# FFN2's activation block sums on GpSimd instead of VectorE, its weight sums on VectorE from two plain loads

## The chip, the cores and the metric

The kernel runs on one core of a Trainium2 chip. The metric is the device time of one execution in microseconds, as a median of several. The core has five engines that run on their own and wait for each other by semaphores: TensorE (PE in the profile), VectorE (DVE), ScalarE (ACT), GpSimd (POOL) and SyncE (SP), which only issues DMAs here.

## The reference

One layer of a hybrid decoder on 1024 tokens of width 1024 (16 meta tokens are put in front). The change touches only the last product.

```
u = rmsnorm(h, g_pre_mix);  z = u @ w_in                 # q | k | v | x | y
attn = sliding_window_attention_with_sinks(q, k, v)      # window 128
rec  = gelu(y) * rg_lru(conv(x))
h = h + rmsnorm(concat(attn, rec) @ w_out, g_post_mix)
u = rmsnorm(h, g_pre_ffn)
f = square(relu(u @ w_ff1)) @ w_ff2                      # w_ff1 1024x4096, w_ff2 4096x1024
h = h + rmsnorm(f, g_post_ffn)                           # returned without the meta tokens
```

## The kernel before, in words

All large products are made in three passes: a float32 operand is split into a high half and a low half (both in the format fp32r), and `mm3` adds high x high, high x low and low x high in PSUM (lines 124, 125 and 126). `split` makes the halves: ScalarE copies the operand into the high half (line 95), VectorE subtracts that from the operand for the low half (line 98).

FFN2 (`w_ff2`) is done by a scheme that replaces eight block products by seven. The activations are kept as four blocks, `fb["11"]`, `["12"]`, `["21"]` and `["22"]`, each of eight tiles 128x(2x512), and `w_ff2` is cut into four blocks in the same way. Each of the seven rows of `PLAN` names which activation blocks are added or subtracted (a single name, or two and an operation), which weight blocks, and into which halves of the result (`facc`) the product goes with which sign. A row is a product `i` from 0 to 6, and it has eight steps `q`, one for each 512 rows of the inner dimension. So there are 56 steps. In each, TensorE makes 24 matmuls of 128x128 by 512 columns (four accumulators of one PSUM bank each, for four groups of 128 tokens, two slices of the inner dimension, three passes); `q` = 7 finishes a product. Block sums of the activations stand in products 0, 1, 2, 5 and 6. Weight sums stand in products 1 to 4 and 6, as ADD in 1, 2 and 6 and as SUB in 3 and 4.

For step `n` the kernel does this ahead:

- `fetch_2(n)`, three steps ahead: the one or two weight blocks are loaded, 512 KB each, into a slot with the tag `raw` and one with the tag `e`, in turns (two slots of each tag). Plain loads are issued by SP (line 1125). For most steps with ADD (`q % 3 < 2` in products 1 and 2, `q` in 0, 2, 4 in product 6) the second block is not loaded into a slot of its own: GpSimd issues a DMA that adds it to the first in memory (`accum_op=ADD`, line 1122).
- `prep_2(n)`, one step ahead: where two blocks were loaded, VectorE combines them (`combine`, line 861). The weight is split into a pair with the tag `ws` (four slots, that is two steps; the last three steps use slots with the tag `a`). Where the plan asks for it, VectorE makes the activation sum, also by `combine`, into a slot with the tag `b`, which is then split into two more slots of that tag. There are 17 slots with the tag `b`, part of which are held by the activation blocks and by `facc`.
- `step_mm` runs the matmuls. The last three steps (`LAST`) are run group by group of tokens instead.

When a product is done, `evict` adds its four accumulators to `facc`, one each in the first four steps of the next product: a first write goes by ScalarE, a later one by VectorE (a sum of a PSUM bank and an SBUF tile of 128x512, line 861). In products 5 and 6 the finished rows are normalized and added to the output: `finish_early` (ScalarE squares, GpSimd a power for the reciprocal root, `rs`, line 169, VectorE a product, line 1191, GpSimd an accumulating DMA to the output, line 1195), `finish_half` and, at the end, `finish_late` (its last product on GpSimd is line 1244, its reductions on VectorE are line 1229, its output DMAs on GpSimd line 1238).

The order of the instructions on each engine is not written out. A list scheduler with a model of the chip's times makes it when the program is built, from the dependences, the slots of the pools and a few ordering hints (`behind`). After that each engine works through its own fixed order, so an instruction that waits holds up all that stand behind it on its engine.

Of the kernel before, what the change touches and what calls it, by code (L numbers as in the profile page):

```python
# [37 lines left out]
def hybrid_layer(  # L38
# [6 lines left out]
    nc = tc.nc  # L45
# [12 lines left out]
    def slot(tag, shape, dt=F32):  # L58
        uid[0] += 1
        return slab.tile(shape, dt, tag=tag, name=f"{tag}{uid[0]}", bufs=bufs[tag])  # L60

    def pair(tag, shape):
        return slot(tag, shape, F32R), slot(tag, shape, F32R)
# [29 lines left out]
    def split(hi, lo, src, eng=None):  # L93
        if eng is None:
            nc.scalar.copy(hi, src)  # L95
        else:
            eng.tensor_copy(hi, src)
        low = nc.vector.tensor_tensor(lo, src, f32(hi), op=ALU.subtract).ins  # L98
        mark[0] = low.name
        return low  # L100
# [4 lines left out]
    def behind(name, *inss):  # L105
        for ins in inss:
            tc.add_manual_dep(
                ins, name,
                mybir.DependencyInfo(
                    mybir.DependencyClass.NoSync, mybir.DependencyReason.DATA  # L110
                ),
                reason="order",
            )
# [157 lines left out]
    def high_w(raw, tag="ws"):  # L271
        hi, lo = pair(tag, [P, KC, P])
        chained(0, nc.scalar.copy(hi, raw).ins)
        return hi, lo
# [59 lines left out]
    wx = high_w(rx)  # L334
# [525 lines left out]
    def combine(dst, x0, x1, op):  # L860
        return nc.vector.tensor_tensor(dst, x0, x1, op=op).ins  # L861
# [79 lines left out]
    fb = {k: [None] * 8 for k in ("11", "12", "21", "22")}  # L941
# [158 lines left out]
    w2v = w_ff2.rearrange("(q s a p) (b c) -> q a b p s c", s=2, a=2, p=P, b=2)  # L1100
    ADD, SUB = ALU.add, ALU.subtract
# [11 lines left out]
    def fetch_2(n):  # L1113
        i, q = steps[n]
        wx = PLAN[i][1]
        tags = (("raw", "e"), ("e", "raw"))[n % 2]
        raws = []
        for (a, b), tag in zip(wx[:2], tags):
            if len(wx) == 3 and wx[2] is ADD and raws and (
                q % 3 < 2 if i < 6 else q in (0, 2, 4)  # L1120
            ):
                nc.gpsimd.dma_start(raws[0], w2v[q, a, b], accum_op=ADD)  # L1122
                break
            r = slot(tag, [P, 2, 512])
            nc.sync.dma_start(r, w2v[q, a, b])
            raws.append(r)
        return raws

    def prep_2(n, tag="ws"):
        i, q = steps[n]  # L1130
        fx, wx, _ = PLAN[i]
        raws = raw_2.pop(n)
        if len(raws) == 2:
            ins = combine(raws[0], raws[0], raws[1], wx[2])
            if i == 6:
                behind(w_low[0], ins)
        wh, wl = pair(tag, [P, 2, 512])
        w_low[0] = split(wh, wl, raws[0]).name
        if len(fx) == 3:
            f = slot("b", [P, 2, 512])  # L1140
            combine(f, fb[fx[0]][q], fb[fx[1]][q], fx[2])
        else:
            f = fb[fx[0]][q]
        fh, fl = pair("b", [P, 2, 512])
        split(fh, fl, f)
        return fh, fl, wh, wl
# [9 lines left out]
    for n, p in enumerate(third):  # L1156
        if n + 2 < 16:
            raw_c[third[n + 2]] = fetch_c(third[n + 2])
        if n >= 13:
            raw_2[n - 13] = fetch_2(n - 13)  # L1160
        if n + 1 < 16:
            wc[third[n + 1]] = prep_c(third[n + 1])
        if n == 15:
            ready[0] = prep_2(0)
        if p not in a12_early:
            y2 = bank(("acc", "s")[p % 2])
            product(y2, wc[p][0], ob21, True)
            nc.vector.tensor_tensor(block("11", p), y2, block("11", p), op=ALU.add)
        y4 = bank(("pt", "o")[p % 2])
        if n == 0:  # L1170
            product_by_parts(y4, wc[p][1], ot4)
        else:
            product(y4, wc[p][1], ot4, True)
        nc.vector.tensor_tensor(block("21", p), y4, block("21", p), op=ALU.add)
        done.add(p)
        if p ^ 1 in done:
            activate("11", p // 2)
            activate("21", p // 2)
# [110 lines left out]
    for n, (i, q) in enumerate(steps):  # L1289
        if n + 3 < len(steps):  # L1290
            raw_2[n + 3] = fetch_2(n + 3)
        if n + 1 < len(steps):
            late = w_low[0]
            ready[n + 1] = prep_2(n + 1, "a" if n + 1 >= len(steps) - LAST else "ws")
        if q == 0:
            old = None if i == 0 else accs
            accs = [[bank(("acc", "s", "pt", "o")[j])] for j in range(4)]
            if i == 6:

                evict(5, 0, old[0][0], late)  # L1300
                accs[3] = [accs[3][0][:, :256], bank("acc")[:, :256]]
        if n < len(steps) - LAST:
            for j in range(4):
                for acc, cols in zip(accs[j], col_parts(i, j)):
                    step_mm(acc, j, q, ready[n], cols)
            del ready[n]
        if old and (q > 0 or i < 6) and q < 4:
            evict(i - 1, q, old[q][0], late)
        if i == 5 and q == 0:
            gffn_b = slot("a", [P, D])  # L1310
            nc.scalar.dma_start(gffn_b, g_post_ffn[0].partition_broadcast(P))
        if (i, q) in EARLY:
            finish_early(EARLY.index((i, q)))
        if i == 6 and 1 <= q < 5:
            finish_half(q - 1)
        if i == 6 and q == 4:
            root = small.tile([P, 1], F32, name="root", tag="root")
            lut(root, half_pow, AF.Sqrt, scale=-1.0)
# [36 lines left out]
```

## Time and profile before

| | |
|---|---|
| median of 3 runs | 976.04 us (975.72 to 976.45) |
| the profiled execution | 983.92 us, its span 982.2 us |
| TensorE clock granted, mean | 0.991 of full speed |
| busy share of the span: PE, PEld, DVE, ACT, POOL | 97%, 81%, 67%, 51%, 14% |
| HBM read, written | 110.46 MB, 18.87 MB |

The profiled execution is slower than the runs by 0.8%; numbers from the trace are compared among themselves. FFN2's matmuls run from about 661 us to 972 us of the span. In the rows of the profile, `out<-in` are the names of the tiles without their numbers: `ws<-raw,ws` on line 98 is the low half of a weight, `b<-b,b` on line 98 the low half of an activation sum, `b<-a,c` on line 861 an activation sum, `e<-e,raw` and `raw<-raw,e` on line 861 a weight sum, `b<-ps_pt,b` an eviction. A time in brackets is idle time of the engine just before the instruction, with what ended it. "Chain" is the chain of work that ended last, followed back from the end.

### The profile page before, as it was taken

To read this page: it belongs to the slowest core of one execution; us is meant where nothing else is said; L and a number is where in the kernel's file an instruction comes from. 1 tells how busy PE (TensorE), PEld (TensorE's weight loads), DVE (VectorE), ACT (ScalarE), POOL (GpSimd) and SP (SyncE) were. 2 spreads that over 40 slices of the span, in tenths; PEclk is the share of its full clock that TensorE was granted. 3 is DMA by queue.
4 is the path that set the end of the run, shared out by engine and by line. 5 is a ranking of instruction groups with operands and counts; after the bars stand their busy time and mean duration, and the time that the engine had idled before them with its cause. 6 is when DMAs were issued, how large, how long until landed. Compare 5 with 4: busy or idle time off the path is not lost.

```text
span 982.2 us, 12324 instructions
## 1 busy us (share of the span) xinstructions
PE 951.9 (97%) x4654; PEld 797.1 (81%) x4654; DVE 662.9 (67%) x942; ACT 500.5 (51%) x816; POOL 140.3 (14%) x184
## 2 busy tenths in 40 slices
PE   6999989999899999999999999999999999999996
PEld 6998988888788887887788888888888788888885
DVE  5569976755876687656554455468567666779885
ACT  6556562548935554343455556555433343445432
POOL 4016753230002100000000000000011000003011
PEclk9999989999999999999999999999999999999999
DMA  8111001112234465575532264423678766656653
GB/s 282 49 46 42 22 23 44 33 43 65 86 107 150 150 215 192 172 243 192 187 129 86 85 200 121 129 86 108 164 180 194 166 222 207 177 168 150 168 175 85
DMA packets 84794, 131.30 MB, mean 134 GB/s; under 512 B 5464, under 2 KB 48616, under 8 KB 84736
## 3 DMA queue, kind: packets, MB, share of 16 engines
q1 hardware_dynamic: 76912, 109.55, 34.7%
q0 software_dynamic: 7248, 19.40, 9.7%
q10 hardware_dynamic: 576, 1.57, 0.4%
q8 instruction: 36, 0.59, 0.3%
q14 instruction: 22, 0.18, 0.1%
HBM read 110.46 MB, written 18.87 MB: 132 GB/s over the span
## 4 chain that ended last, share of the span: by engine, by line
PE 80%; DVE 7%; ACT 5%; DMA 3%; issue 3%; POOL 2%; DVEq 0%; SPq 0%; ACTq 0%; POOLq 0%
PE ps_acc L124 8%; PE ps_acc L125 8%; PE ps_acc L126 8%; PE ps_pt L125 6%; PE ps_pt L126 6%; PE ps_pt L124 6%; PE ps_s L126 6%; PE ps_s L125 6%; PE ps_s L124 6%; PE ps_o L125 5%; PE ps_o L124 5%; PE ps_o L126 5%; DMA d<-in_w_ff_dram 2%; ACT c L82 1%; DVE ws L98 1%
## 5 line engine op out<-in xcount | busy, mean ns | idle before, releaser
L95 ACT CAST ws<-raw 128x1024 fp32r<-128x1024 f32 (+1 forms) x70 | 71.7, 1024 | 128.1 <-PE ps_o L125 47.5
L98 DVE TENSOR_TENSOR ws<-raw,ws 128x1024 fp32r<-128x1024 f32 (+1 forms) x71 | 85.0, 1197 | 46.4 <-ACT ws L95 46.3
L124 PE MATMUL ps_acc<-a,ws 128*128 128x256 f32 (+2 forms) x256 | 87.6, 342 | 1.4 <-ACT d L394 1.3
L125 PE MATMUL ps_acc<-a,ws 128*128 128x256 f32 (+2 forms) x256 | 86.9, 339 | 0.0
L126 PE MATMUL ps_acc<-a,ws 128*128 128x256 f32 (+2 forms) x256 | 86.2, 337 | 0.0
L98 DVE TENSOR_TENSOR b<-b,b 128x1024 fp32r<-128x1024 f32 (+2 forms) x48 | 57.6, 1200 | 26.3 <-PE ps_o L125 20.1
L95 ACT CAST ws<-e 128x1024 fp32r<-128x1024 f32 x42 | 43.9, 1045 | 59.2 <-PE ps_o L125 35.0
L95 ACT CAST b<-b 128x1024 fp32r<-128x1024 f32 (+2 forms) x48 | 49.5, 1030 | 39.0 <-DVE b L861 38.1
L98 DVE TENSOR_TENSOR ws<-e,ws 128x1024 fp32r<-128x1024 f32 x42 | 51.3, 1222 | 16.1 <-ACT ws L95 16.1
L124 PEld LDWEIGHTS ps_acc<-a,ws 128*128 128x128 f32 x256 | 50.1, 196 | 6.1 <-ACT d L394 1.7
L169 POOL TENSOR_TENSOR rs<-ms,half_pow 128x1 f32<-128x1 f32 (+1 forms) x31 | 22.8, 739 | 221.3 <-DVE ms L165 219.9
L575 POOL TENSOR_SCALAR_AFFINE_SELECT c<-c 128x512 fp32r<-128x512 f32 x64 | 49.7, 794 | 27.9 <-ACT c L95 12.5
L126 PEld LDWEIGHTS ps_acc<-a,ws 128*128 128x128 f32 x256 | 49.9, 195 | 4.5
L125 PEld LDWEIGHTS ps_acc<-a,ws 128*128 128x128 f32 x256 | 50.1, 196 | 4.0
L1122 POOL DMA_DIRECT2D raw<-in_w_ff_dram x9 | 11.0, 1218 | 265.5 <-DVE ws L98 206.0
L125 PE MATMUL ps_acc<-ws,b 128*128 128x512 f32 (+1 forms) x120 | 46.2, 385 | 1.2 <-DVE ws L98 1.2
L126 PE MATMUL ps_acc<-ws,b 128*128 128x512 f32 (+1 forms) x120 | 46.3, 386 | 0.0
L124 PE MATMUL ps_acc<-ws,b 128*128 128x512 f32 (+1 forms) x120 | 46.2, 385 | 0.0
L125 PE MATMUL ps_pt<-ws,b 128*128 128x512 f32 x112 | 44.1, 394 | 0.0
L126 PE MATMUL ps_pt<-ws,b 128*128 128x512 f32 x112 | 44.1, 393 | 0.0
L124 PE MATMUL ps_pt<-ws,b 128*128 128x512 f32 x112 | 44.0, 393 | 0.0
L124 PE MATMUL ps_s<-ws,b 128*128 128x512 f32 x110 | 43.4, 395 | 0.0
(388 smaller groups left out, 2740.0 us busy)
## 6 DMA issues: line engine op xcount, KB each, us to landing
raw<-in_w_ff_dram SPq DMA_DIRECT2D x66, 512.0 KB, 4.2
e<-in_w_ff_dram SPq DMA_DIRECT2D x47, 512.0 KB, 3.7
raw<-in_w_in_dram SPq DMA_DIRECT2D x12, 512.0 KB, 4.6
d<-in_w_ff_dram SPq DMA_DIRECT2D x12, 512.0 KB, 4.8
s_dram<-d POOLq DMA_DIRECT2D x12, 512.0 KB, 4.1
raw<-in_w_ff_dram POOLq DMA_DIRECT2D x9, 512.0 KB, 6.6
c<-in_x_dram SPq DMA_DIRECT2D x8, 512.0 KB, 8.1
d<-in_x_dram SPq DMA_DIRECT2D x8, 512.0 KB, 3.5
```

What stands on the lines that cost most here:

```text
L82: ins = nc.scalar.activation(*args, **kwargs).ins
L95: nc.scalar.copy(hi, src)
L98: low = nc.vector.tensor_tensor(lo, src, f32(hi), op=ALU.subtract).ins
L124: nc.tensor.matmul(dst, lh, rh, start=start, stop=False, skip_group_check=True)
L125: nc.tensor.matmul(dst, lh, rl, start=False, stop=False, skip_group_check=True)
L126: last_mm[0] = nc.tensor.matmul(dst, ll, rh, start=False, stop=stop, skip_group_check=True).ins.name
L169: last_pow[0] = nc.gpsimd.tensor_tensor(rs[:n], ms[:n], half_pow[:n], op=ALU.pow).ins.name
L575: nc.gpsimd.affine_select(out=m[:, :, side, :], in_=f32(m)[:, :, 1, :], pattern=[[0, 4], [-sign, P]], compare_op=op, fill=0.0, base=0, cha ...
L1122: nc.gpsimd.dma_start(raws[0], w2v[q, a, b], accum_op=ADD)
```

## The change

All activation sums of FFN2 are made by GpSimd with a `tensor_tensor` of the same tiles. The accumulating loads of weights are gone: in all steps with two weight blocks both are loaded by SP into slots of their own, and VectorE combines them. The matmuls, the splits and the evictions are the same, and so is the code ahead of FFN2. The scheduler makes its order anew from the changed program.

```diff
@@ fetch_2
         tags = (("raw", "e"), ("e", "raw"))[n % 2]
         raws = []
         for (a, b), tag in zip(wx[:2], tags):
-            if len(wx) == 3 and wx[2] is ADD and raws and (
-                q % 3 < 2 if i < 6 else q in (0, 2, 4)
-            ):
-                nc.gpsimd.dma_start(raws[0], w2v[q, a, b], accum_op=ADD)
-                break
             r = slot(tag, [P, 2, 512])
             nc.sync.dma_start(r, w2v[q, a, b])
             raws.append(r)
@@ prep_2
         w_low[0] = split(wh, wl, raws[0]).name
         if len(fx) == 3:
             f = slot("b", [P, 2, 512])
-            combine(f, fb[fx[0]][q], fb[fx[1]][q], fx[2])
+            nc.gpsimd.tensor_tensor(f, fb[fx[0]][q], fb[fx[1]][q], op=fx[2])
         else:
             f = fb[fx[0]][q]
         fh, fl = pair("b", [P, 2, 512])
```

## The prediction

> **What bounds the kernel now.** I read the page first, then the windows cut at the seven products of FFN2, then the chain of waits.
>
> ```profile
> span 982.2 us, 12324 instructions
> PE 951.9 (97%) x4654; PEld 797.1 (81%) x4654; DVE 662.9 (67%) x942; ACT 500.5 (51%) x816; POOL 140.3 (14%) x184
> ```
> ```profile
> core 0: us, PE busy (x) PEld busy (x) DVE busy (x) ACT busy (x) POOL busy (x), PEclk, DMA share, GB/s
> 661.00:705.00 44.00, 44.00 (x192) 35.72 (x191) 28.84 (x25) 19.76 (x21) 2.49 (x2) 1.00 0.46 121
> 705.00:749.00 44.00, 44.00 (x192) 35.73 (x191) 31.22 (x28) 19.89 (x23) 7.21 (x6) 1.00 0.80 184
> 749.00:795.00 46.00, 44.84 (x194) 36.15 (x193) 30.98 (x29) 18.69 (x20) 4.83 (x4) 1.00 0.72 188
> 883.00:927.00 44.00, 44.00 (x192) 35.80 (x191) 39.59 (x43) 21.39 (x30) 9.94 (x9) 1.00 0.65 155
> ...
> 866.00:961.00 95.00, 95.00 (x443) 78.67 (x443) 81.65 (x84) 42.02 (x56) 14.08 (x13) 1.00 0.59 156
> ```
> ```profile
> 585.09 2.77 PE ps_pt L1092 x12
> ...
> 782.27 0.76 issue
> 783.03 1.23 DVE ws L98
> 784.31 0.51 PE ps_acc L125
> ```
>
> PE is busy in every microsecond of FFN2 from 661 on, at full clock, except 1.16 us of the third window (44.84 of 46.00). That hole is the piece at 782 in the chain: PE waits for VectorE's low half of a weight. So, the tail apart, work taken off VectorE can win 1.2 us here and no more; the rest of the change can only cost, where VectorE or GpSimd comes to hold PE up. VectorE is not idle: 28.8 to 39.6 us of each 44.
>
> The pace to be kept is that of one step (24 matmuls). A ScalarE cast of a weight starts when PE leaves the buffers of two steps before, so two casts four steps apart give it; the cadence of VectorE in product 3, which already makes every weight sum itself from two plain loads, stands beside them:
>
> ```profile
> 811.24 1.05 ACT L95 CAST ws<-raw 128x1024 fp32r<-128x1024 f32 x1 [3.56 <-issue]
> 833.36 1.05 ACT L95 CAST ws<-raw 128x1024 fp32r<-128x1024 f32 x1 [3.56 <-issue]
> ```
> ```profile
> 803.64 0.68 DVE L861 TENSOR_TENSOR b<-ps_pt,b 128x512 f32<-128x512 f32 x1
> ...
> 810.93 1.23 DVE L861 TENSOR_TENSOR e<-e,raw 128x1024 f32<-128x1024 f32 x1 [1.74 <-DMA e<-in_w_ff_dram]
> 812.07 1.22 DVE L98 TENSOR_TENSOR b<-b,b 128x1024 fp32r<-128x1024 f32 x1
> 813.20 1.22 DVE L98 TENSOR_TENSOR ws<-raw,ws 128x1024 fp32r<-128x1024 f32 x1
> 815.66 1.23 DVE L861 TENSOR_TENSOR raw<-raw,e 128x1024 f32<-128x1024 f32 x1 [1.24 <-DMA raw<-in_w_ff_dram]
> ...
> 834.45 1.22 DVE L98 TENSOR_TENSOR ws<-raw,ws 128x1024 fp32r<-128x1024 f32 x1 [1.86 <-ACT ws L95]
> ```
>
> (833.36 - 811.24) / 4 = 5.53 us per step, 44.2 us per product. VectorE's large operations start 1.14 us apart. With sum, activation split and weight split it needs 3 x 1.14 = 3.42 us, then 1.24 us pass until the next load, whose buffer that weight split had freed, has landed: 4.7 us, inside 5.53. The split at 834.45 ends at 835.67; PE comes to its weight at 833.36 + 5.53 = 838.89, so it is 3.2 us early.
>
> **What the change moves.** By the plan, block sums stand in products 0, 1, 2, 5 and 6: 40 of 128x1024 go from VectorE to GpSimd, in the same order. Accumulating loads are 6 + 6 + 3 = 15; each becomes a plain load on SP's queue and one more sum on VectorE. PE's and ScalarE's work stays.
>
> *A block sum on GpSimd.* The trace has only half that size:
>
> ```profile
> L559 POOL TENSOR_TENSOR c<-c 128x512 f32<-128x512 f32 x16 | 22.6, 1413 | 51.9 <-ACT c L82 51.8
> L682 POOL MEMSET e<- 128x1024 f32 x1 | 1.0, 951 | 0.0
> L252 POOL MEMSET km<- 128x512 f32 x1 | 0.5, 524 | 0.0
> L861 DVE TENSOR_TENSOR b<-a,c 128x1024 f32<-128x1024 f32 x15 | 18.3, 1220 | 0.5 <-PE ps_o L125 0.5
> ```
> ```profile
> L559 POOL TENSOR_TENSOR c<-c x16: 1268/1298/2387, 65.9 to 198.8; 128x512 f32<-128x512 f32 x16
> ```
>
> Twice the undisturbed 1298 ns is 2.60 us, the upper bound; a memset of twice the size takes 951 / 524 = 1.81 times as long, and 1.81 x 1.298 = 2.36 is the lower. I take 2.4, against 1.22 on VectorE. The Trainium skill (GPSIMD Engine Reference, Performance versus the Vector engine) gives 4497 ns for 2048 elements with two inputs; half, 2.25 us, is an estimate by that page, and would lower each step below by 0.15 us.
>
> *Do the two engines work beside each other?* Here lies the case:
>
> ```profile
> 191.97 1.30 POOL L559 TENSOR_TENSOR c<-c 128x512 f32<-128x512 f32 x1 [0.55 <-ACT c L82]
> 192.87 1.48 DVE L98 TENSOR_TENSOR ws<-raw,ws 128x1024 fp32r<-128x1024 f32 x1 [0.37 <-ACT ws L95]
> ...
> 88.50 1.23 DVE L98 TENSOR_TENSOR ws<-raw,ws 128x1024 fp32r<-128x1024 f32 x1
> 89.19 1.70 POOL L559 TENSOR_TENSOR c<-c 128x512 f32<-128x512 f32 x1 [0.57 <-ACT c L82]
> ```
>
> GpSimd's sum ran to 193.27; the VectorE split that began under it ended at 194.35, 1.08 us later: it did all its work after GpSimd's. In the other pair VectorE was first, to 89.73, and GpSimd ended 1.16 us later, at 1.70 instead of 1.30. So they take turns: a whole operation with two SBUF operands on one holds up such a one on the other. Beside operations that read PSUM GpSimd is not held up. The Trainium skill (SBUF — State Buffer, SBUF: two separate sides) states this as an exclusive lock held for the whole instruction; these rows agree with it, and it speaks against the change: without it the sums would cost only GpSimd's time, with it they use up VectorE's turns. If the engines did not take turns, VectorE's 3.4 us and GpSimd's 2.4 would each fit into a step, and the account below would come to -0.7.
>
> So the common turns per step count: 2.3 us for a block sum (2.4 less the 0.14 by which 1.16 was shorter than 1.30) and 1.14 for each large VectorE operation, against 5.53.
>
> - Product 0 (sum; two splits): 2.3 + 2.28 = 4.6. Fits; hidden by PE.
> - Products 1 and 2 (sum; weight sum; two splits): 2.3 + 3.42 = 5.7, 0.19 over, 16 x 0.19 = 3.0 us. Four evictions of 0.68 in product 2 read PSUM and can lie under GpSimd's turn; if none does, 5.7. The lead: GpSimd's sum is released by the same end of a PE step as the ScalarE cast, so a weight split starts 2.3 instead of 1.1 us behind it, and 3.2 us of lead become 2.0. That leaves 1.0 to 3.7. If no block sum fills the 1.24 us of waiting for the load, each step takes 6.96, and 16 x 1.43 - 2.0 = 20.9 are lost. A sum takes the `b` slot that an activation half of three steps before held (17 slots, of which `fb["11"]` and `facc` hold nine, three used per step), so it may start two steps ahead of its use and will often stand ready when the gap opens: I take 3.5, near the low end.
> - Products 3 and 4: no block sum, as before.
> - Products 5 and 6 with their run-up, 866 to 961: VectorE's 81.65 less 16 x 1.14 plus 3 x 1.14 is 66.8; with 16 x 2.3 for GpSimd 103.6 in 95.0, 8.6 over if nothing overlaps. Sixteen evictions of 0.68 (10.9 us) can lie under GpSimd's turns. I take three quarters of them (8.2), since VectorE's order puts them in pairs behind a weight split, where the load gap is: 0.4 over. Add half of the load gaps in product 6 (8 x 0.62 = 5.0), take off the lead of 2.0: 3.4. With all evictions covered it is 0.7, with none 11.6. Behind GpSimd's waiting `rs` and output DMAs in finish_early stand the next block sums, behind these VectorE's activation splits, and the weight split after them; for this I go up to 4.0.
>
> *The hole at 782.* It came from a weight sum at the head of VectorE's queue, ahead of the split that PE wanted:
>
> ```profile
> 781.89 1.23 DVE L861 TENSOR_TENSOR raw<-raw,e 128x1024 f32<-128x1024 f32 x1 [4.11 <-DMA e<-in_w_ff_dram]
> 774.48 0.37 SPq L1125 DMA_DIRECT2D e<-in_w_ff_dram  x1
> 773.50 1.22 POOL L1122 DMA_DIRECT2D e<-in_w_ff_dram  x1 [4.81 <-DVE b L861]
> e<-in_w_ff_dram SPq DMA_DIRECT2D x47, 512.0 KB, 3.7
> ```
> The plain load took 781.89 - 774.48 = 7.4 us instead of 3.7, with an accumulating load issued 1 us ahead of it on the same DMA engines. With plain loads throughout, the cadence of product 3 holds, where PE never stopped: -1.2, or nothing.
>
> *The 15 loads.* SP gets 15 more issues; as sums in product 3 the 15 on VectorE are in the account above. The accumulating issues leave GpSimd's queue: no gain on PE.
>
> *The tail.* GpSimd's last product moves behind its second output issue:
>
> ```profile
> 970.51 0.95 POOL L1238 DMA_DIRECT2D out_dram<-a  x1 [0.16 <-issue]
> 971.16 1.62 POOL L1244 TENSOR_TENSOR a<-a,a 128x512 f32<-128x512 f32 x1
> 972.41 1.22 POOL L1238 DMA_DIRECT2D out_dram<-a  x1
> ...
> 971.10 1.97 DVE L1229 CUSTOM_DVE_ANT_0 a<-a,late 128x256 f32<-128x256 f32 x1
> 975.11 0.48 DVE L1229 CUSTOM_DVE_ANT_0 a<-a,part 128x256 f32<-128x256 f32 x1
> ```
> It holds up L1229 by 1.97 - 0.48 = 1.5 us today, on the chain. Starting up to 1.2 later it holds up another operation: between -1.0 and +1.5, I take +0.5.
>
> **Sum:** 3.5 + 4.0 - 1.2 + 0.5 = +6.8 us. The profiled execution took 983.92 (its span and 1.7 around it), 7.9 above the median of the runs, 976.04; FFN2 should scale in neither, so 990.7 there and 982.8 as a median.
>
> **Rivals.** *Hidden after all*: the block sums fall into VectorE's waits for loads and casts and PE never stops. It decides at a sum of 5.53 - 3.42 = 2.1 us; for it speaks that VectorE has 13 us idle in product 1, against it 2.36. Then -1.2 + 0.5: 975.3, not slower. *Turns at the wrong place*: GpSimd gets its turn between VectorE's two splits, and the load gap stays empty in products 1 and 2: 20.9 in place of 3.5, 1000.2. It wins over my case where more than about half the gap stays empty; against it, the sums are released early; for it, VectorE's order is fixed and a split waits for its own block sum. *Faster*: the hole goes, the last product's new place takes 1.0 off the tail, nothing stops: 973.8.
>
> **Chances.** Forecast (2 to 14 us slower) 0.58; wrong place 0.18; hidden 0.18; faster 0.06. A measurement of this kernel can tell 0.2%, 2 us, from no change. So faster 0.06, same 0.18, slower 0.76. The range takes in most of the hidden case and half of the wrong-place case, and leaves out the rest of them and the faster one, under 2 in 10: 974.8 to 1001.
>
> **What would show it.** Right: GpSimd rows of 2.3 to 2.6 us and longer, VectorE splits well above 1.22 in products 1, 2, 5, 6 and not in 3, 4; PE holes there behind L98, in sum 8 us; none near 782. Wrong: 40 sums of 2.4 with splits at 1.22 (no turns), or PE without holes, or holes that end at ScalarE or a DMA.

## The result, and the profile after

The changed kernel takes 1001.75 us (median of six runs, 1000.83 to 1004.78); the kernel before, run beside it, 976.25. The ratio is 1.0263, 95% interval 1.0244 to 1.0283: 25.5 us slower. The prediction had 982.8 and a range up to 1001, so the direction was right and the size far too small. The profiled execution took 1004.78, the slowest of the six.

The page of the changed kernel, its first lines, and the line of the waits of PE that is new in FFN2 (the columns: us in total, times, longest):

```profile
span 1003.1 us, 12347 instructions
PE 959.1 (96%) x4654; PEld 797.7 (80%) x4654; DVE 696.8 (69%) x917; ACT 499.5 (50%) x816; POOL 234.0 (23%) x209
```
```profile
PE ps_acc L125 <- DVE ws L98: 16.4, 8, 3.4
```

Eight waits of PE for VectorE's low half of a weight, 16.4 us, in place of one of 1.16. That isn't all of 25.5. The windows, cut as for the kernel before, show the rest:

```profile
core 0: us, PE busy (x) PEld busy (x) DVE busy (x) ACT busy (x) POOL busy (x), PEclk, DMA share, GB/s
661.00:705.00 44.00, 41.05 (x168) 32.39 (x168) 24.80 (x18) 16.48 (x19) 18.74 (x7) 0.96 0.35 108
705.00:749.00 44.00, 40.28 (x162) 32.34 (x163) 36.09 (x21) 16.00 (x18) 17.21 (x6) 0.92 0.53 167
749.00:795.00 46.00, 46.00 (x198) 36.53 (x197) 37.80 (x29) 16.50 (x18) 17.19 (x6) 1.00 0.56 183
795.00:839.00 44.00, 44.00 (x192) 35.73 (x191) 31.66 (x30) 17.89 (x20) 0.00 (x0) 1.00 0.68 212
...
883.00:927.00 44.00, 41.42 (x171) 32.80 (x170) 42.12 (x30) 20.42 (x30) 31.69 (x17) 0.96 0.55 131
```

(The changed kernel enters FFN2 at 653.3 us of its trace, the kernel before at 659.8, so a window does not hold the same steps in both: here product 1 runs from 703.4 to 755.2 and product 2 to 800.2.)

Where PE has holes, PEclk, the granted clock, falls to 0.92 to 0.96 as well; in the windows without holes it is 1.00. In the third window, with the same 17 us of GpSimd's sums, PE is never idle. So the sums cost in some places and nothing in others, and a hole costs more than its length. The second point can be read from the single matmuls behind a hole (start, duration):

```profile
714.54 0.80 PE L125 MATMUL ps_acc<-ws,b 128*128 128x512 f32 x1 [3.20 <-DVE ws L98]
715.13 0.63 PE L126 MATMUL ps_acc<-ws,b 128*128 128x512 f32 x1
715.56 0.63 PE L124 MATMUL ps_acc<-ws,b 128*128 128x512 f32 x1
...
720.52 0.40 PE L126 MATMUL ps_pt<-ws,b 128*128 128x512 f32 x1
720.75 0.40 PE L125 MATMUL ps_o<-ws,b 128*128 128x512 f32 x1
```

For 5.7 us the matmuls start 0.43 us apart, then 0.23 again: half the clock. The window of just this stretch shows the granted clock (the third number from the end) as 0.50:

```profile
714.50:720.30 5.80, 5.76 (x14) 4.51 (x15) 4.62 (x4) 1.04 (x1) 0.00 (x0) 0.50 0.60 184
```

The groups of FFN2 by tile show VectorE's part (count, sum and mean ns):

```profile
L98 DVE TENSOR_TENSOR b<-b,b 128x1024 fp32r<-128x1024 f32 x44 | 76.0, 1732 | 5.0 <-PE ps_o L125 2.9 <-ACT b L95 2.1
L98 DVE TENSOR_TENSOR ws<-e,ws 128x1024 fp32r<-128x1024 f32 x26 | 45.2, 1740 | 8.8 <-ACT ws L95 8.8
L1136 POOL TENSOR_TENSOR b<-a,c 128x1024 f32<-128x1024 f32 x13 | 36.9, 2874 | 85.1 <-issue 67.1 <-PE ps_o L125 10.0 <-DVE b L98 7.0
```

The splits of these two groups, 1.22 us before, take 1.73 on average. Of all splits of FFN2, 16 take 3.3 to 3.5 us, four 2.3 to 2.9 and one 6.39; the rest take 1.2. GpSimd's sums are 2.4 us undisturbed and 2.87 on average in the group shown.

Counted hole by hole (the holes from the end of one matmul to the start of the next; the half clock from the starts behind them that lie 0.3 to 0.7 us apart, less 0.23 each):

| place | predicted | holes | half clock |
|---|---|---|---|
| product 0 | 0 | 2.79, 0.42, 0.25 | 1.5 |
| products 1 and 2 | 3.5 | 1.07, 3.20, all in product 1 | 2.7 |
| products 5 and 6 | 4.0 | 0.17, 2.41, 3.45, 2.78 | 4.8 |
| hole at 782 | -1.2 | gone | |
| tail, from PE's last matmul to the end | +0.5 | 9.65 for 9.78 | |

That is 16.5 and 9.0. From start to start each hole is some 0.2 us longer, and a restart costs 0.1, so the two make 27.9 by the starts, against 1.4 for the one hole before. FFN2 took 340.2 us from PE's first matmul to its last, 312.7 before: 27.5 more in these traces, of which the count explains some 26.5. (That 16.5 and 9.0 add up to just the 25.5 between the medians is chance. The whole trace gained only 20.9, because the execution shown of before was slow in the unchanged work ahead of FFN2, by 6.5 us.)

### The profile page after: what moved, and what is told of

It reads as the page before. It is cut to its first block, busy times and chain, and to the rows that moved or that the text cites. A ratio compares the mean times of both kernels' runs of the same rounds, so it can differ in the third digit from the quotient of the medians.

```text
span 1003.1 us, 12347 instructions
## 1 busy us (share of the span) xinstructions
PE 959.1 (96%) x4654; PEld 797.7 (80%) x4654; DVE 696.8 (69%) x917; ACT 499.5 (50%) x816; POOL 234.0 (23%) x209
## 4 chain that ended last, share of the span: by engine, by line
PE 75%; DVE 12%; ACT 5%; issue 4%; POOL 2%; DMA 1%; DVEq 0%; SPq 0%; ACTq 0%; POOLq 0%
PE ps_acc L125 9%; PE ps_acc L124 8%; PE ps_acc L126 8%; PE ps_pt L125 6%; PE ps_pt L126 5%; PE ps_s L126 5%; PE ps_pt L124 5%; PE ps_s L125 5%; PE ps_s L124 5%; PE ps_o L125 4%; PE ps_o L124 4%; PE ps_o L126 4%; DVE ws L98 4%; DVE b L98 3%; ACT c L82 1%
## 5 line engine op out<-in xcount | busy, mean ns | idle before, releaser
L95 ACT CAST ws<-raw 128x1024 fp32r<-128x1024 f32 (+1 forms) x70 | 71.6, 1023 | 112.9 <-PE ps_o L125 47.2
L98 DVE TENSOR_TENSOR ws<-raw,ws 128x1024 fp32r<-128x1024 f32 (+1 forms) x71 | 94.4, 1329 | 43.5 <-ACT ws L95 43.4
L124 PE MATMUL ps_acc<-a,ws 128*128 128x256 f32 (+2 forms) x256 | 86.5, 338 | 1.4 <-ACT d L394 1.3
L1136 POOL TENSOR_TENSOR b<-a,c 128x1024 f32<-128x1024 f32 x15 | 42.8, 2884 | 184.5 <-PE ps_o L125 109.4
L125 PE MATMUL ps_acc<-a,ws 128*128 128x256 f32 (+2 forms) x256 | 85.8, 335 | 0.0
L126 PE MATMUL ps_acc<-a,ws 128*128 128x256 f32 (+2 forms) x256 | 85.2, 333 | 0.0
L98 DVE TENSOR_TENSOR b<-b,b 128x1024 fp32r<-128x1024 f32 (+2 forms) x48 | 80.4, 1679 | 6.1 <-ACT b L95 3.1
L98 DVE TENSOR_TENSOR ws<-e,ws 128x1024 fp32r<-128x1024 f32 x42 | 64.8, 1544 | 13.9 <-ACT ws L95 13.8
L125 PE MATMUL ps_acc<-ws,b 128*128 128x512 f32 (+1 forms) x120 | 49.1, 409 | 16.4 <-DVE ws L98 16.4
L124 PEld LDWEIGHTS ps_acc<-a,ws 128*128 128x128 f32 x256 | 48.9, 191 | 6.1 <-ACT d L394 1.7
L126 PEld LDWEIGHTS ps_acc<-a,ws 128*128 128x128 f32 x256 | 48.8, 191 | 4.5
L125 PEld LDWEIGHTS ps_acc<-a,ws 128*128 128x128 f32 x256 | 48.9, 191 | 4.0
L126 PE MATMUL ps_acc<-ws,b 128*128 128x512 f32 (+1 forms) x120 | 47.6, 396 | 0.0
L124 PE MATMUL ps_acc<-ws,b 128*128 128x512 f32 (+1 forms) x120 | 47.1, 392 | 0.2 <-ACT ws L95 0.2
L125 PE MATMUL ps_pt<-ws,b 128*128 128x512 f32 x112 | 45.4, 405 | 0.0
L124 PE MATMUL ps_pt<-ws,b 128*128 128x512 f32 x112 | 44.9, 401 | 0.0
L126 PE MATMUL ps_pt<-ws,b 128*128 128x512 f32 x112 | 44.9, 401 | 0.0
```

The lines of the kernel that those rows point to most:

```text
L124: nc.tensor.matmul(dst, lh, rh, start=start, stop=False, skip_group_check=True)
L125: nc.tensor.matmul(dst, lh, rl, start=False, stop=False, skip_group_check=True)
L126: last_mm[0] = nc.tensor.matmul(dst, ll, rh, start=False, stop=stop, skip_group_check=True).ins.name
L1136: nc.gpsimd.tensor_tensor(f, fb[fx[0]][q], fb[fx[1]][q], op=fx[2])
```

## The experiments

**The two halves.** `e1_pool_sums_only` has only the first line of the change, `e2_plain_loads_only` only the second:

```diff
 # e1: as before, but
-            combine(f, fb[fx[0]][q], fb[fx[1]][q], fx[2])
+            nc.gpsimd.tensor_tensor(f, fb[fx[0]][q], fb[fx[1]][q], op=fx[2])
 # e2: as before, but
-            if len(wx) == 3 and wx[2] is ADD and raws and (
-                q % 3 < 2 if i < 6 else q in (0, 2, 4)
-            ):
-                nc.gpsimd.dma_start(raws[0], w2v[q, a, b], accum_op=ADD)
-                break
```

> Half of the change: the 40 block sums by GpSimd, the 15 accumulating loads kept. Theory T (turns): a GpSimd sum of 2.41 us holds up VectorE's next two-operand operation for its whole length, and that alone makes the loss; then this kernel keeps nearly all of the 25.5 us, 994 to 1002. Theory L (loads): the plain loads with their extra weight sums make the chain load, sum, split, next load longer than a step and lose the better part by themselves; then this one is at 976 to 984. Theory B (both): neither alone fills the step, each alone loses under 6 us, and the two losses add to well under 25.5: 977 to 982 here.

> The other half: all weight sums by VectorE from two plain loads, block sums on VectorE as before. T: 974 to 976, since VectorE's five large operations per step take 4 x 1.14 us plus a load gap, and the hole of 1.16 us at 782 goes. L: 990 to 1000, with VectorE waiting 3 to 4.5 us for loads in product 1 as it does in the changed kernel. B: 976 to 982.

Measured: e1 1028.18 (ratio 1.0561, 1.051 to 1.0612), e2 977.19 (1.0014, 0.9997 to 1.0031) beside 975.23. The loads alone are no clear loss, against theory L (theory T had 974 to 976 for them, a little less than measured); but the sums alone cost 53 us, twice the whole change, which no theory had. The queues of e1 show why:

```profile
708.77 1.20 POOL L1122 DMA_DIRECT2D e<-in_w_ff_dram  x1 [9.89 <-DVE ws L98]
717.00 1.21 POOL L1122 DMA_DIRECT2D raw<-in_w_ff_dram  x1 [7.02 <-issue]
717.75 2.83 POOL L1141 TENSOR_TENSOR b<-a,b 128x1024 f32<-128x1024 f32 x1
720.06 2.83 POOL L1141 TENSOR_TENSOR b<-a,c 128x1024 f32<-128x1024 f32 x1
720.62 1.05 ACT L95 CAST b<-b 128x1024 fp32r<-128x1024 f32 x1 [12.86 <-POOL b L1141]
721.70 4.59 DVE L98 TENSOR_TENSOR b<-b,b 128x1024 fp32r<-128x1024 f32 x1 [13.67 <-ACT b L95]
723.64 0.80 PE L124 MATMUL ps_acc<-ws,b 128*128 128x512 f32 x1 [6.60 <-ACT ws L95]
```

An accumulating load waits in GpSimd's queue for 7 to 10 us; the block sums stand behind it and come late and in a bunch. ScalarE waits 12.86 us for the first, with its cast of the next weight behind it in its queue; VectorE is idle for 13.67 us, and PE stops for 6.60, until that weight is cast. So the plain loads, no gain by themselves, save about half of what the sums would have cost.

**What of GpSimd's work it is.** `e3_pool_memset` keeps GpSimd as long busy without reading SBUF, `e4_pool_quarters` cuts the sums:

```diff
 # e3
+            [nc.gpsimd.memset(f, 0.5) for _ in range(3)]
 # e4: for each of four slices c of 256 columns
+                    nc.gpsimd.tensor_tensor(f[:, s_, c], ...[:, s_, c], ...[:, s_, c], op=fx[2])
```

> The changed kernel, but GpSimd fills the tile of the block sum with a constant three times (3 x 0.95 us by the row of before, so about as long as a sum) instead of adding two blocks; the sums are left out. T: these operations read no SBUF operand, so VectorE's splits stay at 1.22 and the time falls to that of the plain loads alone, 974 to 980. If only the lateness of the block sum counts (it ends 2.4 to 2.9 us after its release on either way), nothing changes: 997 to 1003. L: as the plain loads alone, 990 to 1000.

> The changed kernel with each block sum cut into four GpSimd sums of 256 columns. T with whole-instruction turns: a VectorE operation waits for at most one quarter, some 0.7 instead of 2.2 us, and the splits come between the quarters; GpSimd's sum is stretched to some 4 to 5 us; holes of over 2.4 us go: 980 to 992. If VectorE waits until GpSimd's queue is empty, or if the order of work (not the turn) sets the loss, it stays at 997 to 1006. L: 997 to 1003.

Measured: e3 975.1 (1.0003, 0.999 to 1.0016); e4 1003.07 (1.0291, 1.0268 to 1.0313). In e3 PE has no hole in FFN2, and the splits are back at their old length, beside 109.5 us of GpSimd's fills:

```profile
L1136 POOL MEMSET b<- 128x1024 f32 x114 | 109.5, 963 | 220.2 <-PE ps_o L126 107.1 <-PE ps_s L126 67.0 <-DVE b L98 21.0
L98 DVE TENSOR_TENSOR b<-b,b 128x1024 fp32r<-128x1024 f32 x44 | 53.6, 1222 | 25.6 <-PE ps_o L125 15.0 <-ACT b L95 10.5
```

The filled tiles came no earlier than the sums do: ScalarE waits for them 37.3 us in all (20 times), for the sums of the changed kernel 24.0 us (13 times). So the turns at SBUF are the cause, and the later arrival of the block sum is not: theory T. But e4 misses what T expected of short turns (980 to 992) and lies where a VectorE that waits until GpSimd's queue is empty would put it (997 to 1006). One VectorE split waited there through twelve quarter sums, three whole blocks:

```profile
918.69 9.76 DVE L98 TENSOR_TENSOR ws<-e,ws 128x1024 fp32r<-128x1024 f32 x1
918.93 8.43 POOL L1139 TENSOR_TENSOR b<-a,c 128x256 f32<-128x256 f32 x12
928.50 0.79 PE L125 MATMUL ps_acc<-ws,b 128*128 128x512 f32 x1 [9.26 <-DVE ws L98]
```

**Product by product.** Each of these is the changed kernel with `if <condition>:` ahead of GpSimd's sum and the sum on VectorE otherwise: `i == 0`, `i in (1, 2)`, `i in (5, 6)`, and `i == 0 and q > 2`.

> The changed kernel with the block sums on GpSimd in product 0 alone (8 of 40), in the other products on VectorE. In the changed kernel's trace the hole of product 0 is 2.78 us and the half clock behind it costs about 1.5 more. Theory P (each place loses by itself): 979 to 981. Theory C (chained: product 0 eats the lead, and the later products pay for it): the sum of the three kernels with one part each stays well below the 25.5 us of the whole, but this one shows its 4.2, and perhaps new holes in product 1. The prediction's account (2.3 + 2.28 = 4.6 us of turns fit into a step of 5.53): no hole, 975 to 977.

> The changed kernel with the block sums on GpSimd in products 1 and 2 alone (16 of 40). Theory P: 8.1 us by the changed kernel's holes there (4.9 us) and the half clock behind one of them, 982 to 985. Theory C: with VectorE ahead when product 1 begins, hardly any hole, 975 to 978. The prediction's account: 1.0 to 3.7 us, 976 to 979.

> The changed kernel with the block sums on GpSimd in products 5 and 6 alone (16 of 40). Theory P: 13.6 us, 987 to 991, since products 3 and 4 without block sums let VectorE catch up in either kernel, so that nothing of product 0 reaches here; theory C says the same of this one. The prediction's account: 4.0 us, 978 to 981.

> Block sums on GpSimd in product 0 alone, and there only from its fourth step on (5 of 40); the other 35 on VectorE. If product 0's loss came from its first steps (VectorE's split is 2.2 us ahead of PE at the second step, and two splits in a row were held up 2.2 us each): no hole, as the plain loads alone, 975 to 979. If each sum in product 0 costs something anywhere: 978 to 981.

Measured: e5 982.51 (1.0062, 1.0041 to 1.0083), e6 981.09 (1.006, 1.0035 to 1.0084), e7 987.97 (1.0125, 1.0095 to 1.0155), each beside 976.41: 6.1, 4.7 and 11.6 us, together 22.3 of 25.5. So the places lose by themselves, in the main theory P, though e5 lies 1.5 us above P's range and e6 0.9 below it; the prediction's account misses all three, e6 by the least (4.7 us for 1.0 to 3.7).

Not all of this comes from the sums. From PE's last matmul to the end e5, e6 and e11 take 11.3, 11.6 and 11.8 us, as e2 does with the plain loads alone (11.3), where the kernel before has 9.8, the changed kernel 9.7 and e7 8.2. PE's time in FFN2, from the first matmul to the last, leaves that out: beside e2's 311.5 us, e5 takes 317.4, e6 314.6, e7 324.6 and the changed kernel 340.2, which is 5.9, 3.1, 13.1 and 28.7 us more. The places by themselves make 22.1 of 28.7. Most of the rest is in product 1: 51.8 us in the changed kernel, 47.2 in e6, 44.8 in e2. Whether product 0's loss makes product 1 lose more there (theory C), or the half clock that e6 was spared, was not separated.

e11 is 978.15 (1.003, 1.0013 to 1.0046), which lies in both of its ranges; its trace decides. PE has no hole in product 0 and one of 0.93 us in product 1, and FFN2's matmuls take 312.7 us, as in the kernel before: product 0 loses by its first steps alone. These are they, in the changed kernel:

```profile
653.51 4.78 POOL L1136 TENSOR_TENSOR b<-a,c 128x1024 f32<-128x1024 f32 x2 [1.23 <-DVE b L98]
656.03 3.33 DVE L98 TENSOR_TENSOR b<-b,b 128x1024 fp32r<-128x1024 f32 x1 [1.47 <-ACT b L95]
658.88 2.72 POOL L1136 TENSOR_TENSOR b<-a,c 128x1024 f32<-128x1024 f32 x1 [0.59 <-PE ps_o L125]
659.29 3.39 DVE L98 TENSOR_TENSOR ws<-e,ws 128x1024 fp32r<-128x1024 f32 x1
662.73 0.79 PE L125 MATMUL ps_acc<-ws,b 128*128 128x512 f32 x1 [2.79 <-DVE ws L98]
```

Three sums come in 8 us; two splits in a row are held up, 2.1 us each. In the kernel before the same weight was ready 2.2 us ahead of PE:

```profile
662.86 1.22 DVE L98 TENSOR_TENSOR ws<-e,ws 128x1024 fp32r<-128x1024 f32 x1
666.29 0.40 PE L125 MATMUL ps_acc<-ws,b 128*128 128x512 f32 x1
```

**Every other sum**, `if q % 2:` in the same place.

> The changed kernel with every other block sum on GpSimd (odd q, 20 of 40), the others on VectorE. Theory S (each sum costs its own block of 2.2 us): half of the loss, 986 to 990. Theory Q (what costs is sums that come back to back, so that VectorE's next operations wait for two or three of them, or two of its operations are held up in one step): these hardly occur, no hole of 2 us and so no half clock, 975 to 979. Turns counted as capacity: (5.7 + 4.6) / 2 = 5.1 us per step, under 5.53, no loss.

Measured: 986.26 (1.011, 1.0082 to 1.0138), 9.9 us, for half of the sums two fifths of the loss. The number is theory S's. By the trace it is a mixture: of the 10.0 us by which FFN2's matmuls take longer than in e2, 5.1 are lost in product 5, where two sums came back to back after all, behind a DMA issue, and a split took 6.31 us: the case of theory Q. Of the rest 1.0 is lost in product 0 and 3.4 in product 1, without such a wait. There the count of turns by capacity, 5.1 of 5.53 us, is refuted: the average fits, and time is lost nevertheless.

**Products 5 and 6 with GpSimd's queue kept free**: e7 with

```diff
-            o, acc, rstd_of(ssq), gffn_b, op0=ALU.mult, op1=ALU.mult
+            o, acc, ssq[0], gffn_b, op0=ALU.mult, op1=ALU.mult
...
-        nc.gpsimd.dma_start(out[t * P : (t + 1) * P, :], o, accum_op=ALU.add)
+        nc.sync.dma_start(out[t * P : (t + 1) * P, :], o)
```

> The kernel with the block sums on GpSimd in products 5 and 6 alone, but finish_early's work kept off GpSimd's queue: no power for its row scale (another small column takes its place) and the output written by SP without adding, so that part of the computation is changed. Theory Q: the sums no longer queue up behind the waiting power and output issue, so two never run back to back in front of a VectorE split; the hole of 4.64 us goes, and of the 11.6 us about half, 980 to 983. Theory S (each sum's own block): little changes, 985 to 988.

Measured: 988.43 (1.0128, 1.0098 to 1.0158), as e7, near theory S's range and not Q's. The hole of 4.64 us is gone, and so is the split of 6.38 us ahead of it, which began under a DMA issue in e7. But the four holes of e9 (3.18, 1.58, 1.17, 3.07) again make 9 us. `finish_early` in GpSimd's queue is not the cause of the loss there.

**The port and the clock by themselves.** Two small kernels with nothing of the layer in them. `m1_micro` releases six GpSimd sums and eight VectorE operations together, then runs bursts of 40 matmuls with growing waits; `m2_micro` releases four sums and three VectorE subtractions, with different things ahead of them (the lines with the names of m2, loops left out):

```python
nc.gpsimd.tensor_tensor(go[k], va, vb, op=ALU.add)                # the sums
nc.vector.tensor_tensor(vo[k], va, vb, op=ALU.subtract)           # VectorE
nc.gpsimd.tensor_tensor(pw, vb[:, :1], half_col, op=ALU.add)      # m2, in most stretches, ahead of the sums
nc.gpsimd.dma_start(out[:P, :], sent, accum_op=ALU.add)           # m2, in some stretches, behind that line
```

> Two costs by themselves; all of the layer is left out and the output is no result of it. First, six independent GpSimd sums of 128x1024 beside eight independent VectorE operations of the same size, released together: with two SBUF operands, with one, with one in PSUM. Fair turns (the prediction's account): each engine's operations alternate, GpSimd's at 2.3 + 1.14 = 3.4 us apart. Theory Q (GpSimd keeps the port while it has work ready): the first VectorE operation with two operands waits for several sums, up to 6 x 2.4 = 14 us. With one operand, or one in PSUM, VectorE goes on undisturbed in either. Second, bursts of 40 matmuls with waits between them that grow step by step: if a hole of a certain length always halves the clock, there is a sharp bound between 1.2 and 2.4 us; if it depends on where the hole falls, holes of one length come with and without the half clock, and the half clock lasts some 3.4 us or a multiple.

> The port by itself once more; all of the layer is left out and the output is no result of it. Four GpSimd sums of 128x1024 in a row (or sixteen of 256 columns) beside three VectorE subtractions with two SBUF operands, released together by ScalarE. The stretches differ in what GpSimd does just before its first sum (nothing, a power of one column, a power and the issue of a DMA) and in how many short operations from PSUM VectorE does before its first subtraction (0.3 to 2.5 us). Theory Q: where the subtraction begins under GpSimd's DMA issue or power, it waits until all the sums are through (4 x 2.3 = 9.2 us and more), as the 6.3 and 9.8 us waits in the kernels did; elsewhere it waits for one sum. Fair turns: it never waits for more than the rest of one sum, under 3.5 us from begin to end (1.9 beside the sums of 256 columns), whatever came before.

The first of the two lines ahead of the sums is what the expectation for m2 calls a power of one column. It is an addition of one column (0.19 us), so m2 says nothing on a real power.

First the turns. Two stretches of m2, without and with the issue of a DMA ahead of the sums (totals of rows that follow one another):

```profile
31.11 11.20 POOL L87 TENSOR_TENSOR go<-va,vb 128x1024 f32<-128x1024 f32 x4 [4.43 <-ACT vb L79]
33.47 9.93 DVE L114 TENSOR_TENSOR vo<-va,vb 128x1024 f32<-128x1024 f32 x3
...
138.38 0.92 POOL L105 DMA_DIRECT2D out_dram<-sent  x1 [0.37 <-ACT col L75]
138.72 10.92 DVE L114 TENSOR_TENSOR vo<-va,vb 128x1024 f32<-128x1024 f32 x1
139.00 9.55 POOL L87 TENSOR_TENSOR go<-va,vb 128x1024 f32<-128x1024 f32 x4
```

Without it the engines alternate, a subtraction every 3.3 us, as in m1: fair turns, the prediction's 2.3 + 1.14 = 3.4. With it VectorE's subtraction begins under the issue and waits until all four sums are through. This came in five of seven stretches with an issue (10.1 to 10.9 us, once with the subtraction 0.2 us behind the issue's end); in the other two an earlier subtraction still had 0.6 us to go when the first sum came, and they alternated. With only the one-column addition ahead (two stretches) they alternated. So theory Q held behind a DMA issue on GpSimd's queue, and in none of the other stretches; the one stretch of 256 columns behind an issue had a subtraction under way too, and alternated. In e4 an issue at 918.29 stands just ahead of the split of 9.76 us shown above, and one ahead of each of its three other splits of over 3.6. In the changed kernel it happens once, and stands ahead of the hole of 3.45 us:

```profile
920.71 0.90 POOL L1190 DMA_DIRECT2D out_dram<-a  x1 [1.76 <-ACT b L95]
921.34 5.05 POOL L1136 TENSOR_TENSOR b<-a,c 128x1024 f32<-128x1024 f32 x2
921.09 6.39 DVE L98 TENSOR_TENSOR b<-b,b 128x1024 fp32r<-128x1024 f32 x1
```

Then the clock. Bursts of m1 (duration of 40 matmuls, and the wait ahead of them):

```profile
273.17 9.37 PE L115 MATMUL acc<-hr,wr 128*128 128x512 f32 x40 [2.21 <-ACT wr L123]
285.13 10.95 PE L115 MATMUL acc<-hr,wr 128*128 128x512 f32 x40 [2.59 <-ACT wr L123]
313.63 12.27 PE L115 MATMUL acc<-hr,wr 128*128 128x512 f32 x40 [3.49 <-ACT wr L123]
342.54 9.40 PE L115 MATMUL acc<-hr,wr 128*128 128x512 f32 x40 [1.70 <-ACT wr L123]
354.15 10.89 PE L115 MATMUL acc<-hr,wr 128*128 128x512 f32 x40 [2.21 <-ACT wr L123]
```

All seven waits of 0.4 to 1.7 us left 9.4; of three of 2.2 one cost 1.5 more; all eleven of 2.6 to 4.4 cost 1.3 to 2.9 more. So the length alone does not decide it: in the kernels, too, one of 2.02 (e1) brought the half clock, and one of 2.44 (e6) and one of 2.96 (e7) did not.

**Candidates against both kernels.** `e10_plain_loads_tail` is e2 with the last product of the third row block on VectorE (`combine` for GpSimd's operation); `e12_plain_loads_product_2` has the plain loads only where the hole was (`if i != 2 and len(wx) == 3 ...`).

> A candidate against both kernels: plain loads throughout, block sums on VectorE (no hole in PE's work in FFN2), and the last product of the third row block on VectorE too, where it held up a VectorE operation by 1.1 to 1.5 us under GpSimd. By the traces the hole gives 1.2 and the tail 0.4 to 0.8 us: 974 to 975, a ratio of 0.998 to 0.999. If the extra weight sums or the changed order cost something that is not a hole in PE's work: 976 to 978.

> The kernel before, with plain loads and weight sums by VectorE in product 2 alone (6 of the 15 accumulating loads), where its one hole in FFN2 was; block sums on VectorE. A candidate against both kernels. If plain loads take the hole away and the tail stays at the 9.75 us of the kernel before (with plain loads throughout it was 11.4): 1.2 us faster, 974.5 to 975.5 beside 976, a ratio of 0.998 to 1.000. If plain loads lengthen the tail wherever they stand, or cost something that is no hole: 976 to 978.

Measured: e10 978.93 (1.0023, 1.0006 to 1.004), e12 975.78 (0.9999, 0.9981 to 1.0016). Neither beats the kernel before. In e2 PE's holes in FFN2 are down to 0.15 us, but from its last matmul to the end it takes 11.3 us instead of 9.8; that takes back the 1.2 and a little more. In e10 that is 11.6, with one hole of 0.67, and its time lies above both of its ranges. In e12 it is 10.0, with one hole of 0.34. Why the end takes longer stays open; the scheduler orders the last steps anew in each of these kernels. What is left to win is within what the measurement can tell.

## Why the prediction was right or wrong

**Direction and mechanism: right.** The bound is PE, VectorE has no work whose removal is worth anything but one hole, and GpSimd's sums and VectorE's two-operand operations take turns. A sum is 2.40 us undisturbed (2.4 was taken). The turn is 2.14 to 2.3 us and the common period 3.3, as the account had it. Much of what was to be seen was seen: splits of 3.4 us for products 1, 5 and 6 and none between 754 us and the run-up of product 5 at 873, holes at L98, none near 782. But the splits of product 0 were held up too, which was not on the list; in product 2, from 755 on, weight sums were held up (2.0 to 2.6 us) and no split; and the holes make 16.5 us and not 8. *Hidden after all* and *Faster* fell with the 25.5 us.

**The step that failed: averages of turns against a step.** The sum asked whether the turns fit 5.53 us on average. What counts is how far ahead of PE the split is at the moment it is held up, 2.1 us at a time. Product 0 says so most plainly: 4.6 us of turns in 5.53, and a hole of 2.79 us from its first steps, while e11, without the sums of those steps, has none there.

- *Product 0, "4.6. Fits; hidden by PE"*: 6.1 us alone (5.9 in FFN2's matmuls beside e2). The second step's lead was 2.2 us, two splits in a row lost 2.1 each, and the hole of 2.8 brought the half clock. A stage's first steps have less lead than its average, and sums released late come back to back.
- *Products 1 and 2, 3.5*: holes of 4.3 us and 2.7 of half clock; 4.7 alone (3.1 in FFN2's matmuls beside e2). The size is near, but not for the reason given: all of the holes are in product 1. The lead was not 3.2 at the start of product 1: there every step takes two plain loads for the first time, and in e2, without any GpSimd sum, the weight sums come 6.9 us apart for two steps:

```profile
694.43 1.23 DVE L861 TENSOR_TENSOR raw<-raw,e 128x1024 f32<-128x1024 f32 x1 [4.44 <-DMA e<-in_w_ff_dram]
...
701.33 1.22 DVE L861 TENSOR_TENSOR e<-e,raw 128x1024 f32<-128x1024 f32 x1
...
708.15 1.23 DVE L861 TENSOR_TENSOR raw<-raw,e 128x1024 f32<-128x1024 f32 x1 [1.06 <-issue]
```

  That alone runs the lead down to zero at the second step of product 1 (e2's 0.15 us hole), and the next blocked split is a hole of its full length: 2.44 in e6, 3.20 in the changed kernel. "The cadence of product 3 holds" was wrong for these steps. From there on the account was good: in product 2 VectorE's turns set a period of (779.98 - 768.63) / 2 = 5.68 us, for which 5.7 was predicted, and PE is fed just in time:

```profile
768.63 2.15 DVE L861 TENSOR_TENSOR raw<-raw,e 128x1024 f32<-128x1024 f32 x1 [0.60 <-DVE b L861]
...
779.98 2.06 DVE L861 TENSOR_TENSOR raw<-raw,e 128x1024 f32<-128x1024 f32 x1 [1.29 <-DMA raw<-in_w_ff_dram]
```

- *Products 5 and 6, 4.0*: 8.8 us of holes and 4.8 of half clock; 11.6 alone. The mis-sized term is the cover: three quarters of 10.9 us of evictions (8.2) were to lie under GpSimd's turns, and in e7 as in the changed kernel 3.1 of 10.8 ran beside a sum. The eight evictions in product 6 had none to lie under: in the changed kernel GpSimd's last sum ends at 946.4 us, and they run from 948.6 to 965.6. With 3.1 in place of 8.2 the same account gives 0.4 + 5.1 + 5.0 - 2.0 = 8.5, beside holes of 8.8; the other terms of that sum were not measured one by one. The 0.6 added for `finish_early` in GpSimd's queue was no cause of its own (e9).
- *The half clock was not in the account at all*: 9.0 us, a third of the 27.5 by which FFN2 grew in the trace. The only hole of before, 1.16 us, brought none, and all holes were priced at their length.
- *The hole at 782, -1.2*: it went, and in e2 FFN2's matmuls took 1.2 us less; but the time did not fall, since the end took longer (e2).
- *The tail, +0.5*: nothing (9.65 us for 9.78).

**The rival "turns at the wrong place"** gave 1000.2, near the measured time, by another way: 1.43 us lost in every step of products 1 and 2. Those products lost 7.0 in holes and half clock, all of it at two holes of product 1, and 4.7 alone. The nearness is chance.

## What to carry to other kernels

Before moving work to GpSimd beside VectorE, list for each step how far ahead of its consumer VectorE's result is, the first steps of every stage above all: one held-up operation costs 2.1 us there, whatever the average says. Price a hole of over 2 us in PE's work at its length and up to 2.9 us of half clock more. And look at what stands in GpSimd's queue: a sum behind a DMA issue that waits is as late as that issue, and sums behind an issue can keep VectorE out until the last.

## What the runs showed of the hardware

- A hole in PE's work of 2.0 to 2.6 us can halve the clock and from 2.6 us nearly always did (in m1 all eleven, in the kernels one of 2.96 did not); up to 1.9 none did. It lasts about 3.4 us (eight starts 0.43 apart) or twice that. The Trainium skill (TensorE: Matmul & The Clock Gate, What's actually happening) has a free-running window of about 3.4 us, after an idle one of which the clock is halved; that holes of one length (2.21 us) came with and without the half clock, and the 3.4 us, agree, but holes well under one window were enough here.
- The turns between GpSimd and VectorE are fair (3.3 us for a sum and a subtraction of 128x1024) except behind a DMA issue on GpSimd's queue, where VectorE waited for four sums in five of seven stretches, up to 10.9 us. The Trainium skill (SBUF — State Buffer, SBUF: two separate sides) has the lock held for one instruction; in these rows VectorE got no turn between the four.
- VectorE operations with one SBUF operand (`tensor_scalar` of 128x1024) were held up too, against what was expected: 2.8 us in m1 beside sums, 0.69 ahead of them. And so was one of 128x1 with two operands in e7, which takes 0.14 us elsewhere:

```profile
889.86 2.95 DVE L165 SCALAR_TENSOR_TENSOR ms<-sq,sq 128x1 f32<-128x1 f32 x1
890.13 2.65 POOL L1137 TENSOR_TENSOR b<-b,a 128x1024 f32<-128x1024 f32 x1
```

  With an operand in PSUM, 128x512, they ran on at 0.68 us beside sums.
